# Four of sixteen k-tile pairs of each MLP's second product by Strassen's algorithm, in one block of four chunks

## The chip, the cores and the metric

The kernel runs on one core of a Trainium2 chip. The metric is the device time of one launch in microseconds (us). A launch uses five engines: TensorE (PE, matmuls; PEld is its load of the stationary operand), VectorE (DVE), ScalarE (ACT), GpSimd (POOL) and SyncE (SP), which issues the DMA transfers.

## What is computed

A decoder trunk of two layers on one sequence of 256 tokens, width 1024, in float32. Layer 0 mixes tokens by block-sparse attention, layer 1 by dilated window attention; each mixer is followed by an MLP, and after each of the four sub-layers the residual is scaled and normalised. The change concerns the MLPs alone:

```python
def sq_relu_mlp(x, w_in, w_out):          # w_in 1024 x 4096, w_out 4096 x 1024
    return jnp.square(jax.nn.relu(x @ w_in)) @ w_out

h = layer_norm(DEEPNORM_ALPHA * h + mix, ln_mix_g[i], ln_mix_b[i])
h = layer_norm(DEEPNORM_ALPHA * h + sq_relu_mlp(h, mlp_w_in[i], mlp_w_out[i]), ln_mlp_g[i], ln_mlp_b[i])
```

## The kernel before

**Precision.** Each float32 operand is split into a high part, rounded to TensorE's float32r format, and the remainder (`split`, L345): ACT copies the high part (L347), DVE subtracts it for the low part (L352). A product is three matmuls: high by high, high by low, low by high. A weight tile of 128 x 1024 thus costs one DMA of 512 KB into a `raw` buffer (five of them), one ACT copy into a `whi` buffer and one DVE subtraction into a `wlo` buffer (nine of each, `NSLOT`). SP waits before a load until a `raw` buffer is free.

**The MLP** (`Mlp.rest`, L932). The hidden width 4096 is cut into eight chunks of 512, that is four k-tiles of 128 each. For a chunk the first product (`mm_wide`, L503) makes four tiles of 128 hidden units by 256 tokens in the four PSUM banks called `tp`, from four `win` weight tiles: 32 matmuls of 512 columns on the high weights and 32 of 256 columns on the low ones. Then `relu_sq_T` (L889) runs for each of the four tiles: ACT copies one half of the bank (L893), DVE adds the other half (L572, which frees the bank), squares the positive part (L579), ACT and DVE split the result into `ahi` and `alo`. Two tiles share a scratch buffer `ta` (three buffers of 128 x 1024).

The second product (`mm_rows`, L552) takes a k-tile of the activations as the stationary operand, for each half m of the tokens (128 tokens), and streams the `wout` tile of 128 x 1024 past it, in two halves of 512 columns. Its sums stay through all 32 k-tiles in the four PSUM banks called `acc`, one for each pair of token half and column half. A k-tile costs 2 x 2 x 3 = 12 matmuls of 128 x 512. The eight banks of PSUM are so used up: four `tp`, four `acc`.

The chunks are interleaved: first product of chunk c+1, second product of chunk c, and so on, so that the relu of a chunk runs while TensorE works on the next. Chunk 0 is made earlier, beside the normalisation of the mixer. The last k-tiles are held back as a tail, in which each bank is finished by itself and the normalisation (`ln_half`, L779) starts on it. That function adds the bank to ALPHA times the residual `xtok` (tiles `tok`).

**What sets the order.** Nothing runs in the order of the code. `Plan` records each operation with an estimated cost, and `Plan.order` (L140) makes one static order for every engine by list scheduling: due times are counted back from TensorE's end, and at each step the ready operation with the earliest due time is taken. DVE may wait 0.2 us for a more urgent operation (`PATIENT`). Loads on SP stay in the order of the code. Each engine then runs its queue strictly in that order.

## Time and profile before

| | |
|---|---|
| median of 3 runs | 559.21 us (559.14 to 559.27) |
| the profiled execution | 559.36 us, of which the span of the trace is 557.5 us |
| mean granted TensorE clock | 0.998 |
| instructions | 9037, of them 3476 matmuls |
| DMA | 105.63 MB, 189 GB/s on average |

The span is the time from the first to the last instruction of the program; 559.36 - 557.5 = 1.86 us lie around it. The page gives for each engine its busy time and share. A matmul of 512 columns is shown with a duration of some 390 ns, but matmuls are pipelined, so the distance from start to start is what it costs. The same holds in a smaller measure for DVE and ACT, whose next instruction may start before the shown end of the one before. Groups are named by their line in the kernel, output tile and input tiles, with buffer numbers left out.

### The profile page before, as it was taken

The page shows a single profiled execution, that of the slowest core. Times are in us where ns is not written, and L with a number is a line of the kernel's source. Part 1 is how long each engine was busy: PE and PEld are TensorE (multiplying, and loading weights), DVE is VectorE, ACT ScalarE, POOL GpSimd, SP SyncE. Part 2 cuts the span into 40 slices and gives each one's busy share as a digit, 9 for nine tenths or more (in the row PEclk, how much of TensorE's full clock was granted, in tenths as well). Part 3 has the DMA queues.
Part 4 walks back from the last instruction along what each step waited for, and adds up shares of the span by engine and source line. Part 5 has one row for each costly group of instructions (what it writes and reads, how often), then busy time and mean ns, then how long its engine had stood idle before and what let it go on. Part 6 is the DMA issues. An engine that isn't in the chain of part 4 may idle for free.

```text
span 557.5 us, 9037 instructions
## 1 busy us (share of the span) xinstructions
PE 549.2 (98%) x3476; PEld 466.9 (84%) x3476; DVE 411.1 (74%) x747; ACT 298.1 (53%) x506; POOL 8.4 (2%) x13
## 2 busy tenths in 40 slices
PE   9999999999999999999999999999999999999994
PEld 7888887888888888888888888878888888888884
DVE  6889999897574764854877999998847548558465
ACT  5758778466453555454434547565654554445400
POOL 0000000010000000000000000010000000000000
PEclk9999999999999999999999999999999999999999
DMA  8993345557766854746534742546849456475002
GB/s 320 344 340 125 115 150 189 190 180 248 251 201 242 260 179 158 243 151 211 183 108 148 244 136 91 171 170 201 300 146 332 150 192 228 152 225 196 31 1 75
DMA packets 30395, 105.63 MB, mean 189 GB/s; under 512 B 3345, under 2 KB 4369, under 8 KB 30353
## 3 DMA queue, kind: packets, MB, share of 16 engines
q1 hardware_dynamic: 29952, 104.87, 55.8%
q8 instruction: 27, 0.44, 0.3%
q10 hardware_dynamic: 400, 0.20, 0.1%
q14 instruction: 16, 0.12, 0.1%
HBM read 104.01 MB, written 1.05 MB: 188 GB/s over the span
## 4 chain that ended last, share of the span: by engine, by line
PE 97%; DMA 1%; DVE 1%; ACT 0%; issue 0%; SPq 0%; DVEq 0%; ACTq 0%
PE acc L356 58%; PE tp L356 37%; PE tp L664 1%; DMA raw<-in_xw_dram 1%; PE tp L681 1%; DVE tok L579 0%; ACT whi L347 0%; SPq L343 0%; ACT xs L347 0%; DVE bst L802 0%; DVE tok L572 0%; DVEq L1270 0%; DVE mv L837 0%; ACTq L347 0%
## 5 line engine op out<-in xcount | busy, mean ns | idle before, releaser
L352 DVE TENSOR_TENSOR wlo<-raw,whi 128x1024 fp32r<-128x1024 f32 (+2 forms) x186 | 220.4, 1197 | 93.1 <-PE tp L356 53.1
L347 ACT ACTIVATE whi<-raw 128x1024 fp32r<-128x1024 f32 (+2 forms) x186 | 187.8, 1038 | 137.0 <-PE acc L356 68.3
L356 PE MATMUL acc<-whi,ahi 128*128 128x512 f32 (+1 forms) x312 | 121.5, 390 | 0.0
L356 PE MATMUL acc<-wlo,ahi 128*128 128x512 f32 (+1 forms) x312 | 120.9, 388 | 0.0
L356 PE MATMUL tp<-xs,whi 128*128 128x512 f32 x448 | 104.4, 390 | 0.0
L356 PE MATMUL acc<-whi,alo 128*128 128x512 f32 (+1 forms) x312 | 102.9, 387 | 0.0
L356 PEld LDWEIGHTS tp<-xs,whi 128*128 128x128 f32 x448 | 83.9, 188 | 17.4
L356 PEld LDWEIGHTS acc<-whi,alo 128*128 128x128 f32 x312 | 58.6, 188 | 12.1
L356 PEld LDWEIGHTS acc<-whi,ahi 128*128 128x128 f32 x312 | 58.7, 188 | 11.8 <-issue 0.3
L356 PEld LDWEIGHTS acc<-wlo,ahi 128*128 128x128 f32 x312 | 58.7, 188 | 11.3
L356 PE MATMUL acc<-xs,whi 128*128 128x512 f32 (+1 forms) x240 | 56.9, 384 | 0.2 <-ACT whi L347 0.2
L356 PEld LDWEIGHTS tp<-xs,wlo 128*128 128x128 f32 x448 | 55.6, 192 | 1.1
L356 PE MATMUL tp<-xs,wlo 128*128 128x256 f32 x448 | 55.9, 283 | 0.0
L356 PEld LDWEIGHTS acc<-xs,whi 128*128 128x128 f32 x240 | 43.7, 192 | 9.9 <-ACT whi L347 1.2
L572 DVE TENSOR_TENSOR ta<-tp,ta 128x256 f32<-128x256 f32 x56 | 21.9, 418 | 22.7 <-ACT ta L893 22.4
L347 ACT ACTIVATE ahi<-ta 128x256 fp32r<-128x256 f32 x56 | 21.9, 412 | 25.2 <-DVE ta L579 25.2
L893 ACT ACTIVATE ta<-tp 128x256 f32<-128x256 f32 x56 | 21.3, 380 | 24.7 <-PE tp L356 24.7
L356 PE MATMUL acc<-xs,wlo 128*128 128x256 f32 x224 | 31.7, 283 | 0.0
L356 PEld LDWEIGHTS acc<-xs,wlo 128*128 128x128 f32 x224 | 29.4, 192 | 0.6
L356 PE MATMUL acc<-whi,xs 128*128 128x512 f32 (+1 forms) x112 | 28.7, 365 | 0.0
L356 PE MATMUL tp<-whi,xs 128*128 128x512 f32 x80 | 25.4, 399 | 0.1
L356 PEld LDWEIGHTS acc<-whi,xs 128*128 128x128 f32 x112 | 19.8, 189 | 3.4 <-issue 0.2
(97 smaller groups left out, 463.5 us busy)
## 6 DMA issues: line engine op xcount, KB each, us to landing
raw<-in_win_dram SPq DMA_DIRECT2D x64, 512.0 KB, 4.6
raw<-in_wout_dram SPq DMA_DIRECT2D x64, 512.0 KB, 4.3
raw<-in_wqk_dram SPq DMA_DIRECT2D x24, 512.0 KB, 4.7
raw<-in_wo_dram SPq DMA_DIRECT2D x14, 512.0 KB, 3.6
raw<-in_wv_dram SPq DMA_DIRECT2D x8, 512.0 KB, 8.1
g<-in_lng_dram SPq DMA_DIRECT2D x4, 512.0 KB, 5.4
b<-in_lnb_dram SPq DMA_DIRECT2D x4, 512.0 KB, 6.6
raw<-in_wv1a_dram SPq DMA_DIRECT2D x4, 512.0 KB, 3.8
```

What stands on the lines that cost most here:

```text
L347: op("ACT", act(n, sbuf=sbuf), lambda: nc.scalar.activation(hi(), src(), AF.Copy), r, whi, keen=keen)
L352: lambda: nc.vector.tensor_tensor(lo(), src(), f32(hi()), op=ALU.subtract), list(r) + list(whi), wlo,
L356: nc.tensor.matmul(out_ap, lhsT, rhs, start=start, stop=stop)
L572: op("DVE", dve(n) + extra, lambda: nc.vector.tensor_tensor(out_ap(), a(), b(), op=alu), r, w)
L664: nc.tensor.transpose(ps.t[:, c : c + P], src(), ident.t)
L681: nc.tensor.transpose(ps.t[:, 32 * i : 32 * i + 32], src()[c, :], ident.t[c, c])
L893: op("ACT", act(S), lambda: nc.scalar.activation(u(), ps.t[:, S:], AF.Copy), [ps], uk)
```

## The change

In chunks 1 and 2 (`WPAIRS`), two neighbouring k-tiles are taken together as a 2 x 2 problem: activations A[k][m] of 128 x 128 by weights B[k][n] of 128 x 512, into the four sums C[m][n]. Strassen's algorithm (in the form with shared sums) needs seven products instead of eight. Four pairs out of the sixteen of each MLP are done so, in both layers.

- **Activation sums** (`side_sums`): for each pair four DVE operations of 128 x 128 in the `ta` buffer, then one split of 128 x 512 into two `e` tiles (buffers of the attention, idle in an MLP).
- **Weight sums** (`load_pair`): two loads as before, then on DVE one addition of 128 x 1024 and two of 128 x 512, in place in `raw` buffers, of which a pair holds three. Four sets of split weights come out: three of 128 x 1024 in `whi`/`wlo` and one of 128 x 512 in `v` tiles (also the attention's). Per pair that is 3.5 tiles split instead of 2. The host lays the two weight tiles out with their column halves exchanged.
- **Products** (`mm_pair`): 7 x 3 = 21 matmuls of 128 x 512 instead of 24. Three of the seven products are added straight into `acc` banks. The other four belong to several sums with different signs; they go into four side banks, which are the four `tp` banks, held through all four pairs.
- **The end** (`settle`): once the last pair is done, one ACT copy and eight DVE operations of 128 x 512 add the side banks to the residual, which is multiplied by ALPHA there already; `ln_half` then multiplies by 1.
- **The block** (`wide_block`): since the `tp` banks are taken, the first products of chunks 1, 2 and 3 now come one after another, then the 16 k-tiles of chunks 0 to 3 in the order of `WORDER` (a digit for the chunk, a digit for the pair in it), then the first products of chunks 4 and 5, and from there chunks alternate as before. Chunk 3's activations sit in the rotation's buffers `rhi` and `rlo`.

The order is again made by `Plan`. Up to chunk 1's relu TensorE's order is unchanged, and so is the kind of every row on DVE and ACT; only, the tiles that are loaded and split there ahead of time are now those of chunks 2 and 3's first products, where before they were chunk 0's `wout` tiles and chunk 2's first product. Two places of the new order follow, both in layer 0 (in the file of the changed kernel the lines of helpers are a few numbers higher: L359 is a matmul, L355 a low part, L583 an addition, L590 a scaled addition).

On TensorE, a k-tile of the second product before. The `acc` banks 260 and 261 hold the first 128 tokens, 262 and 263 the others; `ahi`/`alo` are the activations:

```order
L356 MATMUL acc_260_1862<-whi_319_1859,ahi_264_1899 128x512
L356 MATMUL acc_260_1862<-wlo_320_1897,ahi_264_1899 128x512
L356 MATMUL acc_261_1865<-whi_319_1859,ahi_264_1899 128x512
L356 MATMUL acc_261_1865<-wlo_320_1897,ahi_264_1899 128x512
L356 MATMUL acc_260_1862<-whi_319_1859,alo_265_1910 128x512
L356 MATMUL acc_261_1865<-whi_319_1859,alo_265_1910 128x512
L356 MATMUL acc_262_1876<-whi_319_1859,ahi_264_1899 128x512
L356 MATMUL acc_262_1876<-wlo_320_1897,ahi_264_1899 128x512
L356 MATMUL acc_263_1879<-whi_319_1859,ahi_264_1899 128x512
```

And in the changed kernel the first four of the seven products of the first pair; `e_284`, `e_285` are the split activation sums, `v_354`, `v_355` the half weight tile, `tp_335` the first side bank:

```order
L359 MATMUL acc_261_2104<-whi_348_1920,e_284_1928 128x512
L359 MATMUL acc_261_2104<-wlo_349_1986,e_284_1928 128x512
L359 MATMUL acc_261_2104<-whi_348_1920,e_285_1941 128x512
L359 MATMUL acc_260_2101<-whi_352_1951,ahi_264_1900 128x512
L359 MATMUL acc_260_2101<-wlo_353_2002,ahi_264_1900 128x512
L359 MATMUL acc_260_2101<-whi_352_1951,alo_265_1917 128x512
L359 MATMUL acc_262_2113<-v_354_2017,ahi_264_1900 128x512
L359 MATMUL acc_262_2113<-v_355_2029,ahi_264_1900 128x512
L359 MATMUL acc_262_2113<-v_354_2017,alo_265_1917 128x512
L359 MATMUL tp_335_2164<-whi_348_1920,ahi_264_1900 128x512
L359 MATMUL tp_335_2164<-wlo_349_1986,ahi_264_1900 128x512
L359 MATMUL tp_335_2164<-whi_348_1920,alo_265_1917 128x512
```

Ahead of the first matmul on `tp_335` the queue now holds 33 matmuls of the block: two whole k-tiles of chunk 0 and three products of the pair.

On DVE, before, where the second chunk's banks are read (`tp_311` to `tp_314`):

```order
L352 TENSOR_TENSOR wlo_334_1972<-raw_332_1893,whi_333_1965 128x1024
L352 TENSOR_TENSOR wlo_337_2026<-raw_335_1908,whi_336_1994 128x1024
L572 TENSOR_TENSOR ta_316_2028<-tp_311_1960,ta_316_2028 128x256
L572 TENSOR_TENSOR ta_316_2028<-tp_312_1967,ta_316_2028 128x256
L352 TENSOR_TENSOR wlo_340_2051<-raw_338_1924,whi_339_2000 128x1024
L572 TENSOR_TENSOR ta_317_2053<-tp_313_1974,ta_317_2053 128x256
L572 TENSOR_TENSOR ta_317_2053<-tp_314_1981,ta_317_2053 128x256
```

And in the changed kernel, where the third chunk's first two banks (`tp_328`, `tp_329`) are read; the first of them becomes the side bank `tp_335`:

```order
L583 TENSOR_TENSOR raw_363_2019<-raw_364_2097,raw_362_2009 128x512
L355 TENSOR_TENSOR wlo_368_2122<-raw_364_2097,whi_367_2111 128x1024
L583 TENSOR_TENSOR raw_362_2009<-raw_363_2019 128x512
L355 TENSOR_TENSOR wlo_370_2139<-raw_363_2019,whi_369_2130 128x1024
L355 TENSOR_TENSOR alo_265_1917<-ta_286_1855,ahi_264_1900 128x256
L583 TENSOR_TENSOR raw_375_2151<-raw_373_2087,raw_374_2099 128x1024
L583 TENSOR_TENSOR ta_333_2156<-tp_328_1981,ta_333_2156 128x256
L583 TENSOR_TENSOR ta_333_2156<-tp_329_1989,ta_333_2156 128x256
L590 SCALAR_TENSOR_TENSOR ta_333_2156<-ta_333_2156 128x256 x2
L355 TENSOR_TENSOR rlo_315_2178<-ta_333_2156,rhi_314_2170 128x256
```

The read of a bank now stands behind the additions and splits of two pairs' weights, where before only ordinary splits stood between the reads.

The diff, without the change of `opens` in `mm_rows` (a bank's first matmul overwrites it) and the replacement of ALPHA by `keep` in `ln_half`:

```diff
+WBLOCK = 4
+WPAIRS = ((1, 0), (1, 1), (2, 0), (2, 1))
+WORDER = "00 10 30 11 20 01 21 31"
...
         op("ACT", act(n), lambda: nc.scalar.activation(v.t[:, :n], ps.t[:, :n], AF.Copy), [ps], [v])
         return v
 
-    def act_tiles():
+    def act_tiles(spare=False):
+        if spare:
+            return mk([P, 4, S], F32R, "rhi", 1), mk([P, 4, S], F32R, "rlo", 1)
         return mk([P, 4, S], F32R, "ahi", 3), mk([P, 4, S], F32R, "alo", 3)
+
+    def side_sums(both):
+        hi, lo = mk([P, 512], F32R, "e", 8), mk([P, 512], F32R, "e", 8)
+
+        def h(j, m):
+            return lambda: both.t[:, 512 * j + S + P * m : 512 * j + S + P * m + P]
+
+        def s(i):
+            c = 512 * (i // 2) + P * (i % 2)
+            return lambda: both.t[:, c : c + P]
+
+        hk = [(both, S), (both, 512 + S)]
+        for i, a, b, alu in ((0, h(0, 1), h(1, 1), ALU.subtract), (2, h(0, 0), h(0, 1), ALU.subtract),
+                             (1, s(0), h(0, 0), ALU.subtract), (3, h(1, 0), s(1), ALU.add)):
+            r = [(both, ("s", 0))] if i == 1 else [(both, ("s", 1))] if i == 3 else []
+            tt(P, s(i), a, b, alu, hk + r, [(both, ("s", i)), (both, 512 * (i // 2))])
+        view = lambda t: t.rearrange("p (a c) -> p a c", a=2)
+        split(
+            512, lambda: view(both.t)[:, :, :S], lambda: view(hi.t), lambda: view(lo.t),
+            [(both, ("s", i)) for i in range(4)] + [(both, 0), (both, 512)], [hi], [lo], sbuf=True,
+        )
+        return hi, lo
+
+    def load_pair(src0, src1):
+        a, b, t = [mk([P, 1024], F32, "raw", 5) for _ in range(3)]
+        full = [(mk([P, 1024], F32R, "whi", NSLOT), mk([P, 1024], F32R, "wlo", NSLOT)) for _ in range(3)]
+        last = mk([P, 512], F32R, "v", 4), mk([P, 512], F32R, "v", 4)
+        for r, src in ((a, src0), (b, src1)):
+            dma(lambda r=r: r.t, src, (), [(r, 0), (r, 1)], P * 4096)
+        lo, hi = slice(0, 512), slice(512, 1024)
+
+        def parts(r, w):
+            both = [(r, 0), (r, 1)]
+            split(1024, lambda: r.t, lambda: w[0].t, lambda: w[1].t, both, [(w[0], 0)], [(w[1], 0)], sbuf=True)
+
+        parts(a, full[0])
+        tt(1024, lambda: t.t.rearrange("p (a c) -> p a c", a=2), lambda: a.t.rearrange("p (a c) -> p a c", a=2),
+           lambda: b.t[:, None, lo].broadcast_to([P, 2, 512]), ALU.add, [(a, 0), (a, 1), (b, 0)], [(t, 0), (t, 1)])
+        parts(t, full[1])
+        tt(512, lambda: b.t[:, lo], lambda: t.t[:, lo], lambda: a.t[:, hi], ALU.add, [(t, 0), (a, 1)], [(b, 0)])
+        parts(b, full[2])
+        tt(512, lambda: a.t[:, lo], lambda: b.t[:, lo], lambda: b.t[:, hi], ALU.add, [(b, 0), (b, 1)], [(a, 0)])
+        split(512, lambda: a.t[:, lo], lambda: last[0].t, lambda: last[1].t, [(a, 0)], [(last[0], 0)], [(last[1], 0)],
+              sbuf=True)
+        return full, last
+
+    def mm_pair(act, sums, weights, acc, side, last):
+        (ahi, alo, j), (shi, slo) = act, sums
+        full, tail = weights
+
+        def pure(k, m):
+            t = slice(m * P, (m + 1) * P)
+            return (lambda: ahi.t[:, j + k, t]), (lambda: alo.t[:, j + k, t]), [(ahi, (j + k, m)), (alo, (j + k, m))]
+
+        def mixed(i):
+            c = slice(i * P, (i + 1) * P)
+            return (lambda: shi.t[:, c]), (lambda: slo.t[:, c]), [shi, slo]
+
+        def product(a, w, c0, bank):
+            ah, al, r = a
+            c = slice(c0, c0 + 512)
+            first = opens(bank)
+
+            def go():
+                mm(bank.t, ah(), w[0].t[:, c], first, False)
+                mm(bank.t, ah(), w[1].t[:, c], False, False)
+                mm(bank.t, al(), w[0].t[:, c], False, last and bank in side)
+
+            op("PE", 3 * 0.2268, go, r + [(w[0], 0), (w[1], 0)], [bank])
+
+        p1, p5, p6, p7 = side
+        product(pure(0, 0), full[0], 0, p1)
+        product(mixed(3), full[0], 512, acc[0][1][0])
+        product(mixed(0), full[1], 0, p5)
+        product(mixed(2), full[1], 512, p7)
+        product(mixed(1), full[2], 0, p6)
+        product(pure(1, 0), full[2], 512, acc[0][0][0])
+        product(pure(1, 1), tail, 0, acc[1][0][0])
+
+    def settle(side):
+        p1, p5, p6, p7 = side
+        z = xtok
+        lo, hi = slice(0, 512), slice(512, 1024)
+        u = mk([P, 1024], F32, "ta", 3)
+
+        def scaled(m, c, src, r):
+            n = c.start // 512
+            stt(512, 0, lambda: z[m].t[:, c], lambda: z[m].t[:, c], lambda: ALPHA, src, ALU.mult, ALU.add,
+                [(z[m], n)] + r, [(z[m], n)])
+
+        op("ACT", act(512), lambda: nc.scalar.activation(u.t[:, lo], p1.t, AF.Copy), [p1], [(u, 0)])
+        scaled(0, lo, lambda: p1.t, [p1])
+        tt(512, lambda: u.t[:, lo], lambda: p6.t, lambda: u.t[:, lo], ALU.add, [p6, (u, 0)], [(u, 0)])
+        tt(512, lambda: u.t[:, hi], lambda: p7.t, lambda: u.t[:, lo], ALU.add, [p7, (u, 0)], [(u, 1)])
+        for m in range(2):
+            scaled(m, hi, lambda: p5.t, [p5])
+        scaled(1, lo, lambda: u.t[:, hi], [(u, 1)])
+        for m in range(2):
+            c = (lo, hi)[m]
+            tt(512, lambda m=m: z[m].t[:, hi], lambda m=m: z[m].t[:, hi], lambda c=c: u.t[:, c], ALU.subtract,
+               [(z[m], 1), (u, m)], [(z[m], 1)])
 
     ln = [0]
 
...
                         for m in range(2):
                             mm_rows(acc[m], item, m)
 
+            sums = {}
+
+            def wide_block():
+                side = [psum("tp") for _ in range(4)]
+                left = len(WPAIRS)
+                for c, n in (map(int, x) for x in WORDER.split()):
+                    j = 2 * n
+                    pos = c * 4 + j
+                    if (c, n) in WPAIRS:
+                        left -= 1
+                        mm_pair((*chunks[c], j), sums[c, n], load_pair(wout[i][pos], wout[i][pos + 1]), acc, side, not left)
+                        if not left:
+                            settle(side)
+                    else:
+                        for k in range(2):
+                            item = ((*chunks[c], j + k), load_w(wout[i][pos + k]), pos + k, nkt)
+                            for m in range(2):
+                                mm_rows(acc[m], item, m)
+
             for c in range(nx, NCH):
                 if c == 4:
                     gb = load_gb(2 * i + 1)
                     if i == 0:
                         ropes.append(const(rope1, [P, 2, S], "ropet"))
                         late["m1"] = const(mask1, [P, 2, 512], "m1")
-                chunks[c] = act_tiles()
+                chunks[c] = act_tiles(c == WBLOCK - 1)
                 ws = [load_w(win[i][c * 4 + j]) for j in range(4)]
                 pss = [psum("tp") for _ in range(4)]
                 mm_wide(pss, ws)
...
                     if j % 2 == 0:
                         both = mk([P, 1024], F32, "ta", 3)
                     relu_sq_T(ps, *chunks[c], j, both, j % 2 * 512)
+                    if j % 2 and (c, j // 2) in WPAIRS:
+                        sums[c, j // 2] = side_sums(both)
                 pend.append(c)
-                while len(pend) > 1:
+                if c == WBLOCK - 1:
+                    wide_block()
+                    pend = []
+                while c >= WBLOCK and len(pend) > 1:
                     do_out(pend.pop(0))
             while pend:
                 do_out(pend.pop(0))
...
-    d["wout"] = a["mlp_w_out"].reshape(DEPTH, DFF // P, P, D)
+    wo = np.array(a["mlp_w_out"].reshape(DEPTH, DFF // P, P, D))
+    for c, n in WPAIRS:
+        k = 4 * c + 2 * n
+        p, q = wo[:, k].copy(), wo[:, k + 1].copy()
+        wo[:, k] = np.concatenate([p[:, :, :512], q[:, :, 512:]], axis=2)
+        wo[:, k + 1] = np.concatenate([p[:, :, 512:], q[:, :, :512]], axis=2)
+    d["wout"] = wo
```

More of the change, by code (lines that the diff above doesn't have):

```diff
@@ L550, in mm_xstat, with opens, mm_rows @@
                 )
-    def mm_rows(pieces, item, m, opens=False):
+    opened = set()
+    def opens(acc):
+        new = acc not in opened
+        opened.add(acc)
+        return new
+    def mm_rows(pieces, item, m):
         (ahi, alo, j), w, pos, total = item
-        first, last = pos == 0 or opens, pos == total - 1
+        last = pos == total - 1
         t = slice(m * P, (m + 1) * P)
+        first = {acc: opens(acc) for acc, _, _ in pieces}
         def go():
@@ L559, in go @@
             for acc, c0, n in pieces:
-                mm(acc.t[:, :n], a, w.hi.t[:, c0 : c0 + n], first, False)
+                mm(acc.t[:, :n], a, w.hi.t[:, c0 : c0 + n], first[acc], False)
                 mm(acc.t[:, :n], a, w.lo.t[:, c0 : c0 + n], False, False)
@@ L788, in ln_half @@
         step = min(n for _, _, n in pieces)
+        keep = 1.0 if (ln[0] - 1) // 2 % 2 else ALPHA
         mv = mk([P, 2], F32, "mv", 4)
@@ L804, in ln_half @@
             if last and m == 1 and c0 == 512:
-                stt(512, 0, lambda: z.t[:, 512:], lambda: z.t[:, 512:], lambda: ALPHA, lambda acc=acc: acc.t,
+                stt(512, 0, lambda: z.t[:, 512:], lambda: z.t[:, 512:], lambda: keep, lambda acc=acc: acc.t,
                     ALU.mult, ALU.add, [(z, 1), acc] + prev, [(z, 1)])
@@ L819, in ln_half @@
                 continue
-            stt(n, 0, lambda c=c: z.t[:, c], lambda c=c: z.t[:, c], lambda: ALPHA, lambda acc=acc, n=n: acc.t[:, :n],
+            stt(n, 0, lambda c=c: z.t[:, c], lambda c=c: z.t[:, c], lambda: keep, lambda acc=acc, n=n: acc.t[:, :n],
                 ALU.mult, ALU.add, [(z, c0 // 512), acc] + prev, [(z, c0 // 512)])
@@ L883, in out_and_ln @@
                 for item in items[k:]:
-                    mm_rows([piece], item, m, piece[0].tag == "tp" and item is items[k])
+                    mm_rows([piece], item, m)
             if m == 1 and between:
```

## The prediction

> **What bounds the kernel now.** I read the page first: engines (part 1) and the chain (part 4).
>
> ```profile
> PE 549.2 (98%) x3476; PEld 466.9 (84%) x3476; DVE 411.1 (74%) x747; ACT 298.1 (53%) x506; POOL 8.4 (2%) x13
> ...
> PE 97%; DMA 1%; DVE 1%; ACT 0%; issue 0%; SPq 0%; DVEq 0%; ACTq 0%
> ```
>
> TensorE holds 97% of the chain, so any matmul taken out anywhere is worth its distance to the next, as long as nobody else becomes late. That distance comes from the chain in order of time, in the MLP's steady part (start, length, what):
>
> ```profile
> 147.34 11.09 PE tp L356 x64
> 158.42 10.91 PE acc L356 x48
> 169.33 11.09 PE tp L356 x64
> ```
>
> A second product's 48 matmuls take 10.91 us: 0.2273 us each. A first product takes 11.09 us. The pieces join without a gap, so TensorE does not wait here at all.
>
> Who could become late is DVE. The stretches of the trace (us, then busy time of PE, PEld, DVE, ACT, POOL) and DVE's groups in one period of 22 us (busy, mean ns, idle before):
>
> ```profile
> 147.00:169.00 22.00, 22.00 (x114) 18.86 (x113) 13.44 (x20) 10.98 (x16) 0.00 (x0) 1.00 0.64 209
> ...
> L352 DVE TENSOR_TENSOR wlo<-raw,whi 128x1024 fp32r<-128x1024 f32 x8 | 9.8, 1221 | 8.6 <-PE tp L356 5.9 <-ACT whi L347 2.7
> ```
>
> DVE works 13.4 us of 22 and waits 8.6 us, mostly for TensorE to give buffers back: it is ahead, with 8.6 us in each period to spare. ACT has 11 us to spare.
>
> DVE's durations overlap, so its prices are start to start. In the timeline (start, length):
>
> ```profile
> 157.44 1.22 DVE L352 TENSOR_TENSOR wlo<-raw,whi 128x1024 fp32r<-128x1024 f32 x1
> 158.58 0.75 DVE L572 TENSOR_TENSOR ta<-tp,ta 128x256 f32<-128x256 f32 x2
> ...
> 160.38 0.42 DVE L579 SCALAR_TENSOR_TENSOR ta<-ta 128x256 f32<-128x256 f32 x1
> 160.71 1.22 DVE L352 TENSOR_TENSOR wlo<-raw,whi 128x1024 fp32r<-128x1024 f32 x1
> ...
> 108.94 0.67 DVE L814 SCALAR_TENSOR_TENSOR tok<-tok,acc 128x512 f32<-128x512 f32 x1
> 109.54 0.07 DVE L814 DVE_READ_ACCUMULATOR tok<-tok,acc 128x1 f32 x1
> ...
> 98.32 0.89 DVE L742 TENSOR_TENSOR alo<-tp,ahi 128x128 fp32r<-128x128 f32 x4 [0.56 <-ACT ahi L739]
> ...
> 39.54 0.42 DVE L572 TENSOR_TENSOR ta<-acc,ta 128x256 f32<-128x256 f32 x1
> 39.99 0.69 DVE L572 TENSOR_TENSOR ta<-ta,ropet 128x512 f32<-128x512 f32 x1
> ```
>
> 1024 columns: 1.14 us; 256: 0.33; 512: 0.60; 128: (0.89 - 0.28) / 3 = 0.20, taking 0.28 for the length of one. An operation that needs the result of the one just before starts later: 0.45 instead of 0.33, 0.12 us more.
>
> **What is removed.** Each pair has 21 matmuls instead of 24, and four pairs in each of two layers: 24 matmuls of 512 columns, 24 x 0.2273 = 5.46 us, all on the path. Row and rule differ here. The Trainium skill, "TensorE: Matmul & The Clock Gate", section "Back-to-back issue gap", gives about 131 ns for each matmul of 512 columns in a sustained stream; by it the removal would be worth 3.1 us, and the sum below would end 2.3 us later. That gets no chance as a rival: this trace's 227 ns, the same in every period of the MLP, decide.
>
> **What is added.** On DVE, for each layer: the pairs' splits grow from 8 to 12 wide ones and 4 of 512 (4 x 1.14 + 4 x 0.60 = 7.0 us); weight sums 4 x (1.14 + 2 x 0.60) = 9.4; activation sums 4 x (4 x 0.20 + 0.60) = 5.6; settling 8 x 0.60 = 4.8. Together 26.8 us. On ACT: four more wide copies and nine of 512, by
>
> ```profile
> 154.82 1.04 ACT L347 ACTIVATE whi<-raw 128x1024 fp32r<-128x1024 f32 x1
> 155.76 0.36 ACT L893 ACTIVATE ta<-tp 128x256 f32<-128x256 f32 x1
> ```
>
> 0.94 us for a wide one, start to start, so at most 13 x 0.94 = 12.2 us. The stretch from chunk 2's first product to the end of the block lasts 2 x 11.09 + 180 x 0.2273 = 63.1 us. ACT has half of that, 31 us, to spare. DVE's 26.8 us stand against 63.1 x 8.6 / 22 = 24.7 us to spare and whatever lead it has. So the sum over the stretch decides nothing; the deadlines inside it do.
>
> **Deadlines in layer 0.** Up to chunk 1's relu the work is the old one, so the old trace gives both starting points:
>
> ```profile
> 136.27 0.40 PE L356 MATMUL acc<-whi,ahi 128*128 128x512 f32 x1
> ...
> 137.40 0.42 DVE L572 TENSOR_TENSOR ta<-tp,ta 128x256 f32<-128x256 f32 x1
> ```
>
> TensorE starts chunk 2's first product at 136.27 instead of chunk 0's second, and the block at 136.27 + 2 x 11.09 = 158.45. DVE stands at the last read of chunk 1's banks at 137.40. From there I count DVE's rows in the new order, taking it as never idle, and 0.08 us for each of its waits on itself (between 0, where the needed result is older, and 0.12).
>
> - *First side bank.* It is the 34th matmul of the block: 158.45 + 33 x 0.2273 = 165.95. The bank is free when DVE has read chunk 3's first bank, the 46th row from 137.40: 14 of 1024, 7 of 512, 16 of 256, 9 of 128 columns and 20 waits. The 45 rows before it take 27.0 + 1.6 us; with 0.2 us for DVE's small waits on ACT it starts at 166.2 and ends, 0.42 long, at 166.6. The step from there to TensorE has no row in this trace; I take 0.3 us, by the next spacing of a read of that size (0.33). TensorE then stands still for 166.9 - 165.95 = 1.0 us. The bounds come from DVE's waits on itself: at 0 each there is no standstill, at 0.12 each it is 1.8 us. The second bank's read follows 0.33 later, while TensorE spends 0.68 on the first: no second wait. The third and fourth banks are read 4.5 and 4.8 us after the first, and first written 4.8 and 5.5 us after it: covered.
> - *Last pair.* Its last half tile (`v`) is DVE's 85th row: 49.0 + 2.2 us, ready at 188.7. TensorE wants it as the 155th matmul: 158.45 + 154 x 0.2273 = 193.45. Margin 4.3 to 4.8 us, and more by the 1.0 already waited.
> - *Settling and chunk 4.* DVE settles from 192 to 197; TensorE ends the block at 199.4 and then needs one freed bank after another. Margin 6 us. Chunk 4's low parts come right behind, at 198.5 to 202, and TensorE needs the first 7.3 us into the product.
> - *Loads.* A pair holds three of five `raw` buffers. The tightest load is the last pair's second tile: its buffer is free when DVE has made the second pair's last sum (175.9 in my count), and its own sum stands at 180.7. That leaves 4.7 us, against
>
> ```profile
> raw<-in_wout_dram SPq DMA_DIRECT2D x64, 512.0 KB, 4.3
> ```
>
>   4.3 us to landing. A load that is 1 or 2 us late costs DVE that much, inside the 4.3 us of the last pair. The two rows of the normalisation and two tables that SP issues ahead of chunk 4's weights delay those, with 8 us of cover.
>
> **Layer 1** starts alike:
>
> ```profile
> 396.09 0.40 PE L356 MATMUL acc<-whi,ahi 128*128 128x512 f32 x1
> ...
> 397.22 0.42 DVE L572 TENSOR_TENSOR ta<-tp,ta 128x256 f32<-128x256 f32 x1
> ```
>
> The same 1.13 us apart. But the order reads chunk 3's banks earlier there: the last of the four is the 46th row with only 10 of 1024, read at 422.1, and the side banks want them from 423.7 to 426.5. No wait. The last pair's margin is 5.0 us.
>
> **The sum** for the profiled execution: 559.36 - 5.46 + 1.0 = 554.9. Its own time lies 0.15 above the median of 559.21, so for the median 554.8 us. What this measurement can tell from no change is about 0.2%, 1.1 us.
>
> **Rivals.**
>
> 1. *DVE spaces its operations by their full lengths, and becomes the bound (slower).* Then each costs 0.08 us more: 45 rows make the first bank 3.7 us later, layer 0 stands for 4.7; layer 1's last pair is late by 85 x 0.083 - 5.0 = 2.1. 559.2 - 5.5 + 6.8 = 560.5. It decides at about that price: with 0.07 us more on each operation the saving is just eaten. The row at 157.44 speaks against it: 1.14 between starts at a length of 1.22, and that operation waits for ACT as the new ones do. For it: the additions with a repeated operand and in place are not in the trace, and more of them wait for DVE itself. The Trainium skill, "VectorE: DVE Perf Modes", section "The DRAIN you can't avoid", says that the next operation starts only when the pipeline has emptied; by that rule this rival would be the rule here, though the same page excepts operations that need not be held. Chance 0.06.
> 2. *Buffers or ACT's strict order make DVE idle by 2 to 3 us more in each layer*, by a late load or by a high part queued behind a copy that waits. In layer 0 what falls ahead of the first bank counts whole, the rest hides. 556 to 558. Against it: every wait I followed had cover. For it: five `raw` buffers with three held. Chance 0.17; a further 0.07 that it grows until nothing is left (558.1 to 560.3).
> 3. *The first bank costs nothing*, because DVE loses less than I took: 553.8. Chance 0.1.
> 4. *The change does not do what it says*: the new order has 1794 matmuls of 512 columns in place of 1818. Excluded.
>
> My case has the remaining 0.6. Faster by over 0.2%: 0.6 + 0.17 + 0.1 = 0.87; same 0.07; slower 0.06. The range from 553.7 to 557.6 leaves out rival 1, the far part of rival 2, and little else. My case alone: 554.0 to 555.6.
>
> **What would show it.** Right: 24 matmuls fewer; TensorE's only wait in an MLP of some 1 us for DVE, in layer 0, at the first side bank; the two blocks 40.9 us long each, plus that wait; a DVE that is busy without pause from 137 to 197. Wrong: waits of TensorE for low weights inside the block, a pause before chunk 4, wide additions spaced more than 1.2 us, or a matmul distance in the pairs other than 0.227.

## The result, and the profile after

| | before | after |
|---|---|---|
| median | 559.24 us (559.14 to 559.63, 4 runs) | 553.63 us (553.34 to 554.36, 4 runs) |
| ratio | | 0.990, 95% interval 0.9883 to 0.9918 |
| the profiled execution | 559.36 us, span 557.5 | 553.61 us, span 551.8 |

The change is faster by 5.6 us, 1.0%. The prediction was 554.8 us with a range from 553.7 to 557.6; the median lies 0.07 us under that range.

The page of the changed kernel, engines and chain:

```profile
PE 543.6 (99%) x3452; PEld 461.6 (84%) x3452; DVE 464.5 (84%) x843; ACT 315.4 (57%) x532; POOL 8.4 (2%) x13
...
PE 97%; DMA 1%; DVE 1%; ACT 0%; issue 0%; SPq 0%; DVEq 0%; ACTq 0%
```

24 matmuls fewer, 96 DVE instructions more, 53 us more of DVE's busy time; TensorE's share of the chain is unchanged. Where the time came from is read from the chain in order of time (start, length, what). First before, the first product of chunk 1 in layer 0 and the last long piece of the program:

```profile
127.98 8.45 PE tp L356 x52
...
528.21 18.47 PE acc L356 x87
```

And after, the same two places and what lies between them in the two MLPs:

```profile
127.52 30.65 PE tp L359 x180
158.17 7.51 PE acc L359 x33
...
199.21 22.20 PE tp L359 x128
221.41 10.91 PE acc L359 x48
...
383.93 31.55 PE tp L359 x184
415.48 5.47 PE acc L359 x24
...
456.31 22.20 PE tp L359 x128
...
522.49 18.47 PE acc L359 x87
```

The last piece starts 528.21 - 522.49 = 5.72 us earlier. Of that, 127.98 - 127.52 = 0.46 us were there already at chunk 1's first product, ahead of any removed matmul. So 5.26 us are the change's. The block of layer 0 takes 199.21 - 158.17 = 41.04 us, that of layer 1 456.31 - 415.48 = 40.83; 180 matmuls at 0.2273 us are 40.91. The predicted standstill of 1.0 us in layer 0 is not there. What is left of it is seen in TensorE's timeline, at the 33rd and 34th matmul of the block (start, shown length):

```profile
165.28 0.39 PE L359 MATMUL acc<-v,alo 128*128 128x512 f32 x1
165.61 0.47 PE L359 MATMUL tp<-whi,ahi 128*128 128x512 f32 x1
165.91 0.40 PE L359 MATMUL tp<-wlo,ahi 128*128 128x512 f32 x1
```

The first side bank's matmul starts 0.33 us after the one before it, where 0.23 is the rule: a standstill of 0.10 us. DVE's side of the same moment, from the row at which the prediction started to count to the read that frees the bank:

```profile
136.91 0.42 DVE L583 TENSOR_TENSOR ta<-tp,ta 128x256 f32<-128x256 f32 x1
...
163.72 1.22 DVE L583 TENSOR_TENSOR raw<-raw,raw 128x1024 f32<-128x1024 f32 x1
165.03 0.76 DVE L583 TENSOR_TENSOR ta<-tp,ta 128x256 f32<-128x256 f32 x2
```

The read starts 28.12 us after the first row, instead of the 28.8 predicted, and TensorE starts 0.58 us after the read's start, instead of 0.72.

Single executions begin differently, as 127.98 and 127.52 show. To compare runs by their traces I therefore use one stretch for each layer: from the start of chunk 1's first product to the start of the second product that follows the first products of chunks 4 and 5. In the changed kernel it is 221.41 - 127.52 = 93.89 us in layer 0; in layer 1 the second product starts at 478.51, so 478.51 - 383.93 = 94.58. Before they are 96.42 and 97.28 us. Two executions of the later runs lie far outside all others (676 and 2243 us); the medians contain them, the ratios do not.

### The profile page after: what moved, and what is told of

It reads as the page before. It is cut to its first block, busy times and chain, and to the rows that moved or that the text cites. A ratio compares the mean times of both kernels' runs of the same rounds, so it can differ in the third digit from the quotient of the medians.

```text
span 551.8 us, 9119 instructions
## 1 busy us (share of the span) xinstructions
PE 543.6 (99%) x3452; PEld 461.6 (84%) x3452; DVE 464.5 (84%) x843; ACT 315.4 (57%) x532; POOL 8.4 (2%) x13
## 4 chain that ended last, share of the span: by engine, by line
PE 97%; DMA 1%; DVE 1%; ACT 0%; issue 0%; SPq 0%; DVEq 0%; ACTq 0%
PE acc L359 53%; PE tp L359 41%; PE tp L675 1%; DMA raw<-in_xw_dram 1%; PE tp L692 1%; DVE tok L590 0%; ACT whi L350 0%; SPq L346 0%; ACT xs L350 0%; DVE bst L917 0%; DVE tok L583 0%; DVEq L1415 0%; DVE mv L952 0%; ACTq L350 0%
## 5 line engine op out<-in xcount | busy, mean ns | idle before, releaser
L355 DVE TENSOR_TENSOR wlo<-raw,whi 128x1024 fp32r<-128x1024 f32 (+2 forms) x194 | 228.2, 1198 | 35.8 <-PE tp L359 17.7
L350 ACT ACTIVATE whi<-raw 128x1024 fp32r<-128x1024 f32 (+2 forms) x194 | 197.1, 1039 | 105.0 <-PE acc L359 44.4
L359 PE MATMUL tp<-xs,whi 128*128 128x512 f32 x448 | 104.6, 390 | 0.0
L359 PEld LDWEIGHTS tp<-xs,whi 128*128 128x128 f32 x448 | 83.5, 188 | 17.2 <-DVE ta L583 0.2
L359 PE MATMUL acc<-whi,ahi 128*128 128x512 f32 (+1 forms) x224 | 87.3, 390 | 0.0
L359 PE MATMUL acc<-wlo,ahi 128*128 128x512 f32 (+1 forms) x224 | 86.6, 387 | 0.0
L359 PE MATMUL acc<-whi,alo 128*128 128x512 f32 (+1 forms) x224 | 76.4, 386 | 0.0
L359 PE MATMUL acc<-xs,whi 128*128 128x512 f32 (+1 forms) x240 | 56.5, 381 | 0.1
L359 PEld LDWEIGHTS tp<-xs,wlo 128*128 128x128 f32 x448 | 55.6, 192 | 1.1
L359 PE MATMUL tp<-xs,wlo 128*128 128x256 f32 x448 | 55.9, 283 | 0.0
L359 PEld LDWEIGHTS acc<-xs,whi 128*128 128x128 f32 x240 | 43.0, 189 | 10.1 <-ACT whi L350 0.9
L359 PEld LDWEIGHTS acc<-whi,alo 128*128 128x128 f32 x224 | 42.1, 188 | 8.6
L359 PEld LDWEIGHTS acc<-whi,ahi 128*128 128x128 f32 x224 | 42.1, 188 | 8.5 <-issue 0.3
L359 PEld LDWEIGHTS acc<-wlo,ahi 128*128 128x128 f32 x224 | 42.1, 188 | 8.0
L583 DVE TENSOR_TENSOR ta<-tp,ta 128x256 f32<-128x256 f32 (+1 forms) x60 | 25.3, 438 | 21.3 <-ACT ta L1008 21.0
L350 ACT ACTIVATE ahi<-ta 128x256 fp32r<-128x256 f32 x48 | 18.8, 416 | 22.6 <-DVE ta L590 22.6
L359 PE MATMUL acc<-xs,wlo 128*128 128x256 f32 x224 | 31.6, 283 | 0.0
L359 PEld LDWEIGHTS acc<-xs,wlo 128*128 128x128 f32 x224 | 29.3, 191 | 0.6
L359 PE MATMUL acc<-whi,xs 128*128 128x512 f32 (+1 forms) x112 | 28.7, 365 | 0.0
L359 PE MATMUL tp<-whi,xs 128*128 128x512 f32 x80 | 25.4, 399 | 0.1
L359 PEld LDWEIGHTS acc<-whi,xs 128*128 128x128 f32 x112 | 19.8, 189 | 3.4 <-issue 0.2
```

Source lines behind the costliest of these rows:

```text
L350: op("ACT", act(n, sbuf=sbuf), lambda: nc.scalar.activation(hi(), src(), AF.Copy), r, whi, keen=keen)
L355: lambda: nc.vector.tensor_tensor(lo(), src(), f32(hi()), op=ALU.subtract), list(r) + list(whi), wlo,
L359: nc.tensor.matmul(out_ap, lhsT, rhs, start=start, stop=stop)
L583: op("DVE", dve(n) + extra, lambda: nc.vector.tensor_tensor(out_ap(), a(), b(), op=alu), r, w)
```

## The experiments

Theory A: the gain is 24 matmuls at their full price, and the loss is only what a tight deadline of DVE costs; DVE's load as such costs nothing. Against it stand three rivals: that another part of the change (the block's order) gives some of the gain; that DVE's whole load in the stretch is what decides; and that the 0.10 us is no deadline at all. Twelve runs follow. Times are medians beside the kernel before on the same chip; ratios are given with their 95% interval.

### The changed kernel again

> The changed kernel once more, nothing altered. Theory: the 24 removed matmuls give their whole price, 5.46 us, and the first side bank costs TensorE 0.1 us instead of the 1.0 us predicted, so the median lies near 559.24 - 5.46 + 0.1 = 553.9, and single profiles scatter around that by what the start (the first DMA and the first split) takes in each run, some 0.5 us. Rival: the change gives more than the matmuls removed, in another part (the order of the block, the normalisation), and the median lies at 553.3 or below.

Measured: 554.06 us (before 558.97), ratio 0.9911 (0.9898 to 0.9925). The profiled execution has stretches of 93.90 and 94.58 us, the same as the first within 0.01. Only its start differs: chunk 1's first product begins at 127.81. So the two medians, 553.63 and 554.06, are of one kernel, and against their own kernels before the gain is 5.6 and 4.9 us, around the 5.46 - 0.1 of theory A. The rival's 553.3 did not come.

### The order alone, and one layer alone

```diff
-WPAIRS = ((1, 0), (1, 1), (2, 0), (2, 1))
+WPAIRS = ()
...
-        keep = 1.0 if (ln[0] - 1) // 2 % 2 else ALPHA
+        keep = 1.0 if WPAIRS and (ln[0] - 1) // 2 % 2 else ALPHA
```

> The block of four chunks and its order are kept, but no pair is done by Strassen's algorithm: all 16 k-tiles of the block by 12 matmuls each, no sums, no side banks, no settling. Theory: the order alone is worth nothing, TensorE never waits, 559.0 to 559.5, same as before. Rival: the order saves something by itself (three first products in a row, two at the end of the block): 558.5 or less.

Measured: 559.14 us (before 558.97), ratio 1.0004 (0.9995 to 1.0013). The order of the block is worth nothing, as theory A has it; its stretches are 96.38 and 97.28 us, where the kernel before has 96.42 and 97.28. The chain shows the block whole, 192 matmuls in one piece without a wait:

```profile
158.82 43.55 PE acc L359 x192
...
418.64 43.55 PE acc L359 x192
```

43.55 us against 41.04 and 40.83 after: Strassen's pairs give 2.51 us in layer 0 and 2.72 in layer 1, of the 12 x 0.2273 = 2.73 that each could give. Layer 0's missing 0.2 us stand around the first side bank (0.10 ahead of it, 0.07 after its first matmul). Together 5.23 us.

In the other run the block and its pairs stand in layer 1 only; layer 0 is the old code (each place that builds the block asks for `i == 1`):

```diff
-                if c == WBLOCK - 1:
+                if i == 1 and c == WBLOCK - 1:
                     wide_block()
```

> Block and Strassen's pairs in layer 1's MLP alone; layer 0's MLP is as before the change. Theory: half of the matmuls removed and no wait, 559.24 - 12 x 0.2273 = 556.5. Rival (the two layers do not add, or part of the gain lies outside the pairs): over 557.0 or under 556.0.

Measured: 556.75 us (before 558.97), ratio 0.9959 (0.9947 to 0.9972), 2.2 us less, between the rival's two bounds; layer 1's stretch is 94.60 us, as in the changed kernel, and layer 0's 96.40, as before the change. The layers add.

### More work on DVE: where does it hurt?

Three runs repeat a 128x1024 weight sum, with the result unchanged. The repetition stands inside the step that the planner orders, so that every queue keeps the changed kernel's order:

```diff
+EXTRA = {(1, 0): 1}
...
+        def first_sum():
+            for _ in range(1 + extra):
+                nc.vector.tensor_tensor(
+                    t.t.rearrange("p (a c) -> p a c", a=2), a.t.rearrange("p (a c) -> p a c", a=2),
+                    b.t[:, None, lo].broadcast_to([P, 2, 512]), op=ALU.add)
```

**The first pair's sum twice.**

> Only the first pair's first weight sum (128x1024) is made twice, in one step of the plan, so that every queue keeps the order of the changed kernel: 1.14 us more of DVE in each layer. Theory A (in layer 0 DVE reaches the first side bank with no slack at all, 0.10 us late): TensorE stands still for 0.10 + 1.14 = 1.2 us there and for nothing in layer 1, 1.1 us over the changed kernel, 4.2 under the kernel before. Theory B (the 0.10 us is not a deadline but a gap of its own, and DVE has room): no change, 5.3 under the kernel before.

Measured: 555.44 us (before 559.18), ratio 0.9933 (0.9921 to 0.9946). Stretches 94.64 and 95.47 us: 0.75 more in layer 0 and, against the expectation, 0.89 in layer 1. TensorE's timeline tells where; in layer 0 at the start of chunk 3's first product and at the first side bank, in layer 1 inside chunk 3's first product (in brackets the idle time and what ended it):

```profile
147.47 4.87 PE L360 MATMUL tp<-xs,whi 128*128 128x512 f32 x20 [0.21 <-DVE ta L584]
...
166.01 0.39 PE L360 MATMUL acc<-v,alo 128*128 128x512 f32 x1
166.52 0.47 PE L360 MATMUL tp<-whi,ahi 128*128 128x512 f32 x1
...
405.12 3.81 PE L360 MATMUL tp<-xs,whi 128*128 128x512 f32 x16
409.55 2.79 PE L360 MATMUL tp<-xs,whi 128*128 128x512 f32 x11 [0.62 <-DVE ta L584]
```

And DVE's read for which the last of these waits:

```profile
409.08 0.75 DVE L584 TENSOR_TENSOR ta<-tp,ta 128x256 f32<-128x256 f32 x2
```

Chunk 3's first product takes over the `tp` banks that chunk 2's relu still reads. That is a deadline which the prediction did not list, and 1.14 us more of DVE are enough to miss it in both layers. With 0.2273 us for a matmul of 512 columns, TensorE loses 166.52 - 166.01 - 0.23 = 0.28 us at the first side bank instead of 0.10, and 409.55 - 405.12 - 16 x 0.2273 = 0.79 in layer 1; the rest of layer 0's 0.75, some 0.5 us, lies at 147.47 and in the matmuls right behind it. One sum of 1.14 us costs 0.75 and 0.89 us, so that DVE had slack for the other 0.4 and 0.25 us. Theory B falls, since the bank's wait grows with the sum. Theory A is right that a deadline decides, but had only one of two places: of its 1.1 us more at the side bank 0.2 are there, and it had none in layer 1.

**All four pairs' sums twice** (`{(1, 0): 1, (1, 1): 1, (2, 0): 1, (2, 1): 1}`).

The earlier run that this text names is the first of the next part.

> Each of the four pairs' first weight sum is made twice, again in one step of the plan and with the queues in the changed kernel's own order: 4.56 us more of DVE in each layer. Theory A (deadlines): three sums stand ahead of layer 0's first side bank, 3.4 us; layer 1 loses nothing: 3.4 us over the changed kernel, 1.9 under the kernel before. Theory B (what the earlier run with a repeated sum lost in layer 1, 1.8 us, comes from the load and not from its order, which had moved): 5 us over the changed kernel, the time of the kernel before.

Measured: 558.79 us (before 559.18), ratio 0.9994 (0.9985 to 1.0003): no gain is left that the measurement can tell. The median is the one of theory B; the trace decides between the two. Stretches 97.15 and 95.81 us: 3.26 more in layer 0, as theory A has it (3.4), and 1.23 in layer 1, where it had none. The first side bank, on TensorE:

```profile
165.98 0.39 PE L360 MATMUL acc<-v,alo 128*128 128x512 f32 x1
169.03 0.47 PE L360 MATMUL tp<-whi,ahi 128*128 128x512 f32 x1 [2.67 <-DVE ta L584]
```

and on DVE, the doubled sum and the read for which TensorE waits:

```profile
166.07 2.48 DVE L829 TENSOR_TENSOR raw<-raw,raw 128x1024 f32<-128x1024 f32 x2
168.47 0.75 DVE L584 TENSOR_TENSOR ta<-tp,ta 128x256 f32<-128x256 f32 x2
```

In layer 1 the loss is 0.9 us again at chunk 3's first product, ahead of which only one of the four sums stands, and 0.3 us in chunk 5's. The second sum, ahead of the side banks of layer 1, costs nothing, as the prediction's margin there says. So 4.2 of the 4.5 us fall at two deadlines, the kind of cause that theory A has, though it had only one of the two; 0.3 us are left for the load of theory B, which had 1.8.

**The last pair's sum four times** (`{(2, 1): 3}`).

> The last pair's first weight sum is made four times, the other pairs' once, queues in the changed kernel's order: 3.4 us more of DVE in each layer, all of it behind the first side bank. Theory A (deadlines: the last pair's margin was counted at 4.3 to 5 us): no change against the changed kernel, 5.3 us under the kernel before. Theory B (DVE's whole load against the stretch, as fitted from 4.6 us that cost 1.8): 0.7 us in each layer, 3.9 under the kernel before.

Measured: 554.49 us (before 559.18), ratio 0.9913 (0.9899 to 0.9926). Its chain, layer 0:

```profile
127.72 30.65 PE tp L360 x180
...
221.61 10.90 PE acc L360 x48
```

The stretch is 221.61 - 127.72 = 93.89 us, the changed kernel's own, and 94.62 in layer 1 (94.58). This settles place against load: 3.4 us of DVE behind the first side bank cost nothing in either layer, and three sums ahead of it, 3.4 us as well, cost 3.26.

### The same sums, with the order free to move

An earlier form recorded the repetition as a step of its own, without a cost in the plan:

```diff
+        for _ in range(EXTRA):
+            op("DVE", 0.0, lambda: nc.vector.tensor_tensor(
```

> Each pair's first weight sum (128x1024) is made twice on DVE, with the same result: 4 x 1.14 = 4.6 us more of DVE in each layer, the order unchanged. Theory (the deadline of the first side bank): in layer 0 three of these sums stand ahead of the read that frees the first side bank, so it comes 3 x 1.14 = 3.4 us later and TensorE stands still for 0.1 + 3.4 = 3.5 us there; in layer 1 two stand ahead of the four reads, 2.3 us against a margin of 3.6, no wait: 553.7 + 3.4 = 557.1. Rival (DVE's whole load decides: it has waits enough in the MLP to take 4.6 us): under 554.5. Second rival (both layers lose what is added): 553.7 + 2 x 3.4 = 560.5 or more.

Measured: 559.16 us (before 558.97), ratio 1.0003 (0.9992 to 1.0013). The order did not stay unchanged, as that text has it: the added step moved other rows of DVE and ACT, and six matmuls. Layer 0 lost 2.85 us at the first side bank (3.4 expected). Layer 1 lost 1.82, where none was expected, in waits of 0.1 to 0.5 us between 451 and 480 us. From this run alone I fitted a margin of 2.7 us at the end of the stretch, which stands in the texts of the runs below. The runs above do not bear it out: with the order fixed, the same 4.6 us cost layer 1 1.23, of which 0.3 behind the block, and 3.4 us on the last pair cost 0.04.

Then the same with `WORDER = "00 01 10 11 20 30 21 31"`, and, apart from it, with six `raw` buffers (`NSLOT = 8` for the room):

> As the kernel with the first weight sum made twice, and the block begins with all four k-tiles of chunk 0, so that TensorE reaches the first side bank 24 matmuls, 5.45 us, later. Theory A (a deadline and a margin): layer 0's wait at the first side bank goes, since 2.85 is less than 5.45, but DVE is then as far behind at the end of the block as it is in layer 1, where 4.6 us more cost 1.83 us ahead of chunk 4: both layers lose 1.8 us, 5.46 - 3.7, 1.8 us under the kernel before. Theory B (the first side bank is the only place in layer 0): layer 0 loses nothing, 3.6 us under the kernel before. Theory C (the order of the block does not matter): as without the shift, the same as the kernel before.

Measured: 562.27 us (before 559.03), ratio 1.006 (1.0045 to 1.0075): none of the three theories. Layer 0 lost 2.53 us, layer 1 5.13. In layer 1, TensorE:

```profile
435.24 0.39 PE L360 MATMUL acc<-whi,alo 128*128 128x512 f32 x1
439.11 0.77 PE L360 MATMUL tp<-whi,e 128*128 128x512 f32 x1 [3.48 <-DVE ta L584]
439.68 0.63 PE L360 MATMUL tp<-wlo,e 128*128 128x512 f32 x1
440.10 1.05 PE L360 MATMUL tp<-whi,e 128*128 128x512 f32 x2
440.96 0.63 PE L360 MATMUL tp<-wlo,e 128*128 128x512 f32 x1
```

The wait is again for DVE's read of a `tp` bank. The deadline had moved, but the planner, which knew of the later date and not of the repeated sums' price, had put that read later too, behind more weight sums. It says nothing of the margin. The standstill itself is 439.11 - 435.24 - 0.23 = 3.64 us. The other 1.5 us come right behind it: up to 442.18 the matmuls start some 0.43 us apart instead of 0.23, and the granted clock is 0.69 from 439 to 444 us. Behind the standstill of 2.8 us in layer 0 of the run with all four sums twice the clock stayed at 1.00 (169 to 173 us).

> As the kernel with the first weight sum made twice, with six raw buffers instead of five (and eight pairs of whi and wlo buffers instead of nine, for the room). Theory A (in layer 1 it is the loads that are late, since a load waits for a raw buffer that DVE frees late): the 1.83 us of layer 1 fall under 0.5, the 2.85 of layer 0 stay: 2 us under the kernel before. Theory B (DVE's work itself is too much for the stretch): no change, within 0.5 us of the kernel before.

Measured: 561.64 us (before 559.03), ratio 1.0051 (1.0039 to 1.0063). Inconclusive: stretches 95.19 and 98.50 us, but also 1.3 us more ahead of the first MLP's stretch (of which 0.4 are there at 23 us already) and 1.3 us more between the two, where no sum was added. The eight `whi`/`wlo` buffers are a likely cause, which is not shown, and what the sixth `raw` buffer is worth cannot be told apart from it.

### Fewer sums on DVE

All three weight sums of a pair go to GpSimd: `tt(..., ALU.add, [...], [...], "POOL")`.

> The changed kernel with the three weight sums of each pair on GpSimd instead of DVE: 9.4 us less of DVE in each layer, none of it on TensorE's path. Theory A (TensorE has no wait left but 0.1 us at the first side bank): the same as the changed kernel, 5.2 to 5.5 us under the kernel before. Theory B (GpSimd's sums take much longer than DVE's 1.14 and 0.60 us, the pair's raw buffers are held longer and the loads come late): 1 to 5 us over the changed kernel. Its trace gives GpSimd's price of a sum.

Measured: 563.45 us (before 559.03), ratio 1.0075 (1.0062 to 1.0088). Stretches 97.14 and 100.70, 3.2 and 6.1 us more than the changed kernel's. Taking work off DVE made DVE later. DVE's timeline in layer 0, and GpSimd's beside it:

```profile
143.39 3.90 DVE L583 TENSOR_TENSOR ta<-ta 128x128 f32<-128x128 f32 x3
147.21 0.68 DVE L355 TENSOR_TENSOR e<-ta,e 128x512 fp32r<-128x512 f32 x1
```

```profile
143.08 4.06 POOL L585 TENSOR_TENSOR raw<-raw,raw 128x1024 f32<-128x1024 f32 x2 [26.53 <-DMA raw<-in_wout_dram]
```

Three additions of 128x128, 0.20 us each elsewhere, take 143.39 to 147.21 on DVE, just as long as GpSimd's two sums are running (143.08 to 147.14). The waits of TensorE follow:

```profile
PE tp L359 <- DVE ta L583: 5.6, 5, 2.0
PE tp L359 <- DVE wlo L355: 1.5, 2, 1.0
```

Theory A falls. Theory B has the sign, but not the size: 9.4 to 9.8 us over the changed kernel instead of 1 to 5. Its reason is there in part. TensorE's waits name DVE, and in layer 0 the chain ahead of them is DVE's and ACT's, with no load and no sum of GpSimd; in layer 1 it also holds a load (443.68 us, 5.68 long) and the two sums of GpSimd behind it, to 453.3 us. How the loss divides between stopped DVE rows and late sums is not shown.

### More pairs

`WPAIRS` gets a fifth pair, `(3, 1)`.

> A fifth pair, chunk 3's second, so 6 matmuls fewer in all: 1.36 us less of TensorE. On DVE a pair's splits and sums cost (26.8 - 4.8) / 4 = 5.5 us more. Theory A (4.6 us more cost 1.83 in layer 1, so the margin at the end of the block is 2.7 us): 5.5 less 2.7, and 0.7 for the shorter block, is a wait of 3.5 us in each layer against 0.68 saved: 5.6 us over the changed kernel, the time of the kernel before. Theory B (the margins of 4.3 to 6 us that the prediction counted at the end of the block): a wait of 1 us or none, 1.4 us under the changed kernel to 0.6 over it.

Measured: 552.45 us (before 559.03), ratio 0.9881 (0.9868 to 0.9894). Its chain:

```profile
127.56 30.65 PE tp L359 x180
...
220.76 10.91 PE acc L359 x48
...
383.30 31.55 PE tp L359 x184
...
477.19 10.91 PE acc L359 x48
```

The stretches are 93.20 and 93.89 us, 0.69 less than the changed kernel's in each layer, for three matmuls at 0.2273 = 0.68. The fifth pair gives its full price though it adds 5.5 us to DVE in each layer by the prices above (4.9 by the page's busy time, 474.3 us in all instead of 464.5): its work stands behind the tight deadlines, in layer 0 from 186.72 us on. Theory A of that text, the fitted margin, is refuted; theory B is right.

The last run adds a second block to it: chunks 4 to 6 with the pairs `(6, 0)` and `(6, 1)`, ahead of chunk 7. With it the last k-tiles change: two of chunk 4 and chunk 7's four are left for the end, and the tail is at most six long. The main lines of the edit:

```diff
+WPAIRS2 = ((6, 0), (6, 1),)
+WORDER2 = "40 50 51 60 61"
...
+                if c == NCH - 2:
+                    wide_block(WPAIRS2, WORDER2, 1.0)
+                    pend = []
```

> Seven pairs in each MLP: five in the block of four chunks, as in the run with chunk 3's second pair, and chunk 6's two in a second block of chunks 4 to 6. 18 matmuls fewer than the changed kernel in all, 4.1 us. Theory A (DVE's spare time in chunks 4 to 6, where it waits 8.6 us in each period of 22, pays for the second block's 11 us of splits and sums and 4.8 of settling): 4.1 us under the changed kernel, 9.4 under the kernel before. Theory B (the second settling and the load of the first block meet): 1 to 4 us of waits, 5.4 to 8.4 under the kernel before.

Measured: 550.33 us (before 559.18), ratio 0.9844 (0.983 to 0.9857): the fastest version, 3.3 us under the changed kernel by the two medians and 3.8 by the profiled executions (553.61 and 549.79; 0.3 of that is the start, 127.52 and 127.24). The list of TensorE's waits shows one that is not in the changed kernel's:

```profile
PE acc L361 <- DVE xs L357: 0.5, 1, 0.5
```

Of the 18 x 0.2273 = 4.1 us, 3.5 arrive. The wait stands at 292.69 us, where layer 0's normalisation hands over to layer 1's mixer, and costs TensorE 0.8 us, where the changed kernel loses 0.3; in the blocks the list has none. So theory A is right on the blocks, and the result, 8.8 us under the kernel before, lies between its 9.4 and the best case of theory B, 8.4. Whether the second block's work on DVE or the changed tail makes the wait is not shown. DVE is now busy for 506.1 us, 92% of the span.

## Why the prediction was wrong, and what of it was right

**Right.** TensorE bounds the kernel, and each removed matmul is worth its distance to the next: 2.72 of 2.73 us in layer 1. The order of the block costs and brings nothing. DVE keeps up: it settles from 191.35 to 196.28 (192 to 197 predicted); TensorE ends the block at 199.21 (199.4, in which the standstill was not counted); the last pair's margin and the loads held, and 3.4 us more there did no harm. Deadlines, not DVE's sum over the stretch, decide.

**The step that failed** is the term "TensorE then stands still for 166.9 - 165.95 = 1.0 us" at the first side bank. It measured 0.10. Three things make up the difference of 0.87 us (from 0.97, before rounding). The 45 rows of DVE took 28.12 us instead of 28.8: 0.68. The read hands its bank over 0.58 us after its start instead of 0.42 + 0.3: 0.14. TensorE's own 33 matmuls came 0.05 later against DVE's first row (165.28 + 0.23 - 136.91 = 28.60, where 165.95 - 137.40 = 28.55 was counted).

Behind the 0.68 is DVE's "0.08 us for each of its waits on itself", 20 times, 1.6 us. DVE's timeline after shows what such a wait costs:

```profile
139.51 0.76 DVE L590 SCALAR_TENSOR_TENSOR ta<-ta 128x256 f32<-128x256 f32 x2
140.30 1.02 DVE L583 TENSOR_TENSOR ta<-ta 128x128 f32<-128x128 f32 x4
141.24 0.75 DVE L355 TENSOR_TENSOR alo<-ta,ahi 128x256 fp32r<-128x256 f32 x2
141.91 1.95 DVE L583 TENSOR_TENSOR raw<-raw,raw 128x1024 f32<-128x1024 f32 x2
143.77 0.69 DVE L355 TENSOR_TENSOR e<-ta,e 128x512 fp32r<-128x512 f32 x1
...
145.53 0.76 DVE L583 TENSOR_TENSOR ta<-tp,ta 128x256 f32<-128x256 f32 x2
146.55 0.42 DVE L583 TENSOR_TENSOR ta<-tp,ta 128x256 f32<-128x256 f32 x1 [0.26 <-ACT ta L1008]
...
157.64 1.22 DVE L583 TENSOR_TENSOR raw<-raw,raw 128x1024 f32<-128x1024 f32 x1
158.77 1.22 DVE L355 TENSOR_TENSOR wlo<-raw,whi 128x1024 fp32r<-128x1024 f32 x1
159.91 0.68 DVE L583 TENSOR_TENSOR raw<-raw,raw 128x512 f32<-128x512 f32 x1
160.51 1.22 DVE L355 TENSOR_TENSOR wlo<-raw,whi 128x1024 fp32r<-128x1024 f32 x1
```

Where the operand comes from the row just before, it is 0.12 to 0.14 us: two rows of 256 columns take 0.79 instead of 0.67, four of 128 take 0.94 instead of 0.80, the sums of 1024 and 512 take 1.86 instead of 1.74. Where one row stands between, it is nothing: the sum at 159.91 reads that of 157.64, and 158.77 to 159.91 is 1.14, the plain price. Laid beside the plain prices, the 45 rows are late at five places of this kind, 0.6 us in all instead of 1.6, and at two others: 0.35 us at 146.55, where the profile names ACT, and 0.17 ahead of the read at 165.03, where it names nothing. These two stand for the 0.2 of small waits. Counted so, the working gives 27.0 + 0.6 + 0.5 = 28.1, and the first bank costs 0.1 to 0.3 us (by a handover of 0.58 or 0.72): all but rival 3 of the prediction, which it had priced at 553.8 us and given 0.1. Its bounds (0 to 1.8 us) held; the value inside them was chosen badly, since the prediction already said that a wait costs nothing "where the needed result is older" and then priced all 20 alike without looking which rows stand side by side.

**The range.** With 0.1 in place of 1.0 the sum gives 559.36 - 5.46 + 0.1 = 554.0 for the profiled execution and 553.9 for the median, inside the range. The profiled execution took 553.61, and its start was 0.46 us earlier than before: that the first median fell 0.07 us under the range and the second, 554.06, inside it is luck, as far as the traces show. The low end of 553.7 was rival 3 and nothing below it. It left no room for what one kernel differs by from one measurement to the next: 553.63 and 554.06 for the changed kernel, 558.97 to 559.24 for the one before. In the traces that is the start: chunk 1's first product, with TensorE's order unchanged ahead of it, began at 127.98 before, and at 127.52 and 127.81 in two profiles of the changed kernel; the 0.46 us between the first two are there at 23 us already (22.93 and 22.47 for the same long piece of 86 matmuls).

**Rivals 1 and 2.** DVE's wide operations start 1.14 us apart with a length of 1.22 also in the new rows, those with a repeated operand too (157.64 to 158.77), so rival 1 falls. By the rule of the Trainium skill that was weighed there ("VectorE: DVE Perf Modes", section "The DRAIN you can't avoid") they would start 1.22 apart or more, unless the exception that the page makes holds for them; these rows do not show that spacing. Rival 2's idle DVE did not come: TensorE lost 0.2 us in layer 0 and none in layer 1.

**What the prediction lacked** beside this: the banks that chunk 3's first product takes over. It changed nothing in the result, but the next 1.14 us of DVE ahead of them cost 0.5 us there in layer 0 and 0.9 in layer 1.

**Open.** Why the start differs by up to a microsecond from run to run (that piece of 86 matmuls starts between 22.20 and 23.33 us in the traces); and what of the slower runs with six `raw` buffers is due to the eight `whi`/`wlo` buffers: neither was tried by itself.

## What to carry to other kernels

When an engine stands behind the bounding one with much idle time, do not ask how much work it can take but where: find the places where it hands a buffer over with no slack, and count only the rows ahead of each. Work behind the last such place was free here up to some 5 us in each layer; sums ahead of it, 3.4 us together, cost TensorE 3.26. Price a wait of an engine on itself by whether the needed result comes from the row just before; and let a range end outside the best case by what the same kernel differs between two measurements.

## What the hardware showed that I had not expected

GpSimd's additions in SBUF stop DVE's. While two of them ran, from 143.08 to 147.14 us, three DVE additions of 128x128 took 3.8 us instead of 0.6, and DVE's low parts became longer on average. The groups of the stretch from 138 to 200 us (busy us, mean ns), of the changed kernel and of the one with GpSimd's sums:

```profile
L355 DVE TENSOR_TENSOR wlo<-raw,whi 128x1024 fp32r<-128x1024 f32 x25 | 29.7, 1219 | 0.0
```

```profile
L355 DVE TENSOR_TENSOR wlo<-raw,whi 128x1024 fp32r<-128x1024 f32 x21 | 28.8, 1393 | 0.2 <-ACT whi L350 0.2
```

A sum of 128x1024 takes 2.63 us on average on GpSimd, where DVE's start 1.14 us apart. The Trainium skill, "SBUF — State Buffer", section "Who interferes with whom", says that GpSimd shares a pair of ports with DVE, and that a DVE instruction with two inputs from SBUF contends with a GpSimd instruction that reads SBUF; the stopped additions have two such inputs each, and this run agrees.
